# A transformer trunk on one core: first loads joined, the last stage by token, splits by stock in the gated embedding, and a head's output product in the step of its turn

## The chip, the core and the metric

The kernel runs on one core of a Trainium2 chip. The metric is device time in microseconds; the time of a kernel is the median of its runs. Lines such as L226 are lines of the kernel before; the changed kernel has its own numbers, mostly a little higher.

A core has engines that each take their own instructions strictly in order: TensorE (PE: matmuls and transposes), VectorE (DVE), ScalarE (ACT: functions and copies), GpSimd (POOL) and SyncE (SP: here it only issues DMAs). They wait for one another by semaphores.

## The reference, cut to what matters

256 tokens of 1024 channels pass two layers. Each layer has an FFN, a token mixer, a second FFN and a gated embedding; the mixer is latent attention (MLA) in layer 0 and forgetting attention (FoX) in layer 1, with 8 heads each.

```
h = x
for i in range(2):
    h = h + 0.5 * swiglu(rms_norm(h, ffn_norm[i, 0]), ffn_w_in[i, 0], ffn_w_out[i, 0])
    u = rms_norm(h, mix_norm[i])
    h = h + (mla_mixer(u, ...) if i == 0 else fox_mixer(u, ...))
    h = h + 0.5 * swiglu(rms_norm(h, ffn_norm[i, 1]), ffn_w_in[i, 1], ffn_w_out[i, 1])
    gate = sigmoid(rms_norm(h, ple_norm[i]) @ ple_w_gate[i])
    h = h + gate * (p[i] @ ple_w_proj[i])
return rms_norm(h, final_norm)
```

`swiglu` is `(silu(u @ w_in[:, :2816]) * (u @ w_in[:, 2816:])) @ w_out`. All data are float32.

## The kernel before, in words

**State and precision.** The state h lies transposed in `hT`: 8 blocks (d) of 128 channels by 256 tokens. Every large product is made of three matmuls: weights and inputs are each split in a high part and a remainder, and high·high, low·high and high·low are added (`mm3`, `part`, L210–227). With two halves of the input side by side one weight block takes a matmul of 512 columns (`whi`) and one of 256 (`wlo`).

**Weights.** They stream through one plan in the order of use (class `Weights`, L61–136): SP loads a slab of 512 KB into one of 4 raw tiles, ACT makes `whi` (L97), DVE makes `wlo` (L101), and up to 7 such pairs wait for PE. Each call of `W.pump` (L107) splits one more slab at that place of the program; `catch_up` (L121) does so only if fewer than 4 are in stock. So the calls set where the 1 us pieces of ACT and DVE stand among the other work of these engines.

**Norms.** `Norm` (L252–314) never waits before a product: it multiplies the state by the gain and splits it (`high` on ACT, `low` on DVE, both into `u`), while ACT squares each block and POOL adds the squares up. `by_token` (L297) sums them over partitions on PE (`pst`), and takes the root by a power on POOL (`rtok`); `by_column` (L307) spreads it over partitions on PE (`pb`) and ACT copies it (`rb`). The results are scaled by it only after the product.

**First stage.** L834–846 load: the gains, the state in five pieces and the first four slabs, of which the first comes in two halves, on SP's and ACT's queues; 20 matmuls on zeros follow on PE (L848–852), then the loop of L853–862 splits state and slabs, with one square for each of the 8 blocks. `first` multiplies the first four groups block by block as they arrive.

**Attention** (L405–526). Each step h of a loop works on several heads at once, `lag` steps apart (3 in MLA, 2 in FoX): DVE normalizes the shares of head h−2, PE makes the queries of a later head (`project`), multiplies the shares' transposes with the values of head h−lag−1 (`values`: product `po`, L449/450, whose result is split into `os` by ACT and DVE, L206/207), transposes the shares of head h−lag (`turn`: `pt`, which ACT copies to `ptS`, L442–444) and makes the scores of head h−1 (`psc`), whose maximum DVE takes (`nm`) and whose exps ACT makes (`pr`, L427/428). The output projection is filled in between (`fill`): PE adds the products of finished heads to the first 4 output blocks. A table, `MLA_FILLS` or `FOX_FILLS`, says how many such pairs stand at the first and the second place of each step. The order of the loop body:

```
for h in range(H + lag):
    shares(h - 2); project(h, 0)
    fill_some(fills.get((h, 0), 0))
    values(h - lag - 1); turn(h - lag); scores(h - 1)
    project(h, 1); W.catch_up()
    fill_some(fills.get((h, 1), 0))
    ready = h - lag
values(H - 1)
```

**Gated embedding** (`ple`, L754–831). The embedding of the tokens is projected (`pe`, to `es`), then for each block d PE makes the gate (`ps`), DVE scales it (`zg`), ACT takes the sigmoid, DVE splits the block before (`u`) and one slab (`wlo`), and multiplies and adds. In the last layer the same function also squares the new state, transposes it times the final gain back to token order (`po`, 128 by 512), scales it by the root and stores four pieces of 256 KB from SP (L820–831).

Of the kernel before, what the change touches and what calls it, by code (L numbers as in the profile page):

```python
# [19 lines left out]
P = 128  # L20
# [19 lines left out]
G_KV = 74  # L40


MLA_FILLS = {(6, 1): 3, (7, 1): 3, (8, 0): 3, (8, 1): 4, (9, 0): 4, (9, 1): 4, (10, 1): 3}
# [16 lines left out]
class Weights:  # L60
# [60 lines left out]
    def catch_up(self):  # L121

        if self.loaded < self.got + self.PAIRS - 3:
            self.pump()
# [16 lines left out]
def trunk(ctx, tc, xT, pT, pos, gains, freq, bf, ffn_first, ffn_in, ffn_out, w_down, w_uq, w_ukv, mla_o,  # L141
          fox_qk, fox_v, fox_f, fox_o, ple_gate, ple_proj, out):
# [19 lines left out]
    def plan_ple(i):  # L162
        plan.extend(ple_proj[i, c] for c in range(2))
        plan.extend(ple_gate[i, d] for d in range(KD))
# [8 lines left out]
    plan_ple(0)  # L173
# [6 lines left out]
    plan_ple(1)  # L180


    hT = const.tile([P, KD, T], F32, name="hT")
    g_sb = const.tile([P, 75], F32, name="g_sb")
# [67 lines left out]
    class Norm:  # L252


        def __init__(self, gain, blocks, dim, tag="u"):
            self.gain, self.dim, self.acc, self.left = gain, dim, None, blocks
            if gain is not None:
                bufs = 2 if tag == "u" else 1
                self.pair = act.tile([P, blocks, 2, T], F32R, name=tag, bufs=bufs)
# [15 lines left out]
        def square(self, src, cuts=(slice(0, T),)):  # L275
# [3 lines left out]
            self.left -= 1  # L279
            if self.acc is None:  # L280
                self.acc = sq
            elif self.gain is None and self.left == 0:
                self.rest = sq
# [11 lines left out]
        def by_token(self):  # L295
            pst = psm.tile([P, 2], F32, name="pst", tag="small")
            accs = [self.acc] if self.gain is not None else [self.acc, self.rest]  # L297
            for t in range(2):
                for a in accs:
                    nc.tensor.matmul(pst[:, t:t + 1], a[:, t * P:(t + 1) * P], ones[:, :1],  # L300
                                     start=a is accs[0], stop=a is accs[-1])
# [103 lines left out]
    def attention(project, score, v, scale, nxt, lag, fills, early, cumq=None):  # L405
        os = act.tile([P, H, 2, T], F32R, name="os", tag="u")
# [90 lines left out]
        for h in range(H + lag):  # L497
            if 0 <= h - 2 < H:
                shares(h - 2)
            if h < H:  # L500
                project(h, 0)
            elif h == H:
                W.pump()
            fill_some(fills.get((h, 0), 0))
            if 0 <= h - lag - 1:
                values(h - lag - 1)
            if 0 <= h - lag:
                turn(h - lag)
            if 0 <= h - 1 < H:
                scores(h - 1)  # L510
# [27 lines left out]
    def mla(norm, nxt):  # L538
# [48 lines left out]
        queries(0, 1)  # L587
        W.pump()
        nkv.by_token()
# [164 lines left out]
    def ple(pp, norm, nxt):  # L754
        whole = slice(0, T),

        def gated(d, z, e):
            zg, sg, ge = tmp("zg"), tmp("sg"), tmp("ge")

            final = po and d == KD - 1  # L760
            cuts = (slice(0, P), slice(P, T)) if final else whole
            src = hT[:, d, :]
            for c in cuts:
                nc.vector.tensor_mul(zg[:, c], z[:, c], norm.rb[:, c])
            for c in cuts:
                nc.scalar.activation(sg[:, c], zg[:, c], AF.Sigmoid)
            if not po and d:
                nxt.low(d - 1, hT[:, d - 1, :])
            if d < KD - 1:
                W.pump()  # L770
            for c in cuts:
                nc.vector.tensor_mul(ge[:, c], e[:, c], sg[:, c])
                nc.vector.tensor_add(src[:, c], src[:, c], ge[:, c])
            if po:
                nxt.square(src, cuts)
                hg = work.tile([P, T], F32, name="hg", tag="pr", bufs=4)
                for c in cuts:
                    nc.scalar.activation(hg[:, c], src[:, c], AF.Copy, scale=g_sb[:, G_FIN + d:G_FIN + d + 1])
                hgs.append(hg)
            elif d < KD - 1:  # L780
# [6 lines left out]
        def by_token(d):  # L787
            for t in range(2):
                if d % 4 == 0:
                    po[t].append(bank("po", (P, 4 * P)))  # L790
                nc.tensor.transpose(po[t][d // 4][:, d % 4 * P:(d % 4 + 1) * P], hgs[d][:, t * P:(t + 1) * P], ident)


        hgs = []
        po = ([], []) if nxt.gain is None else None

        es = big.tile([P, KD, T], F32, name="es", tag="big")
        for c in range(2):
            w, = W.get()
            for i in range(4):  # L800
                if i % 2 == 0:
                    pe = bank("pe")
                if (c, i) == (1, 2):
# [7 lines left out]
            W.pump()  # L811
        for d in range(KD):
# [3 lines left out]
            if po and d >= 3:  # L816
                by_token(d - 3)
        if po:
            by_token(KD - 3)
            by_token(KD - 2)  # L820
# [262 lines left out]
```

## Time and profile before

| what | us |
|---|---|
| median of 3 runs | 1010.28 (1009.68 to 1011.18) |
| the profiled execution | 1010.07 |
| its span, first to last instruction | 1008.1 |
| PE busy | 992.8 |
| DVE busy | 745.9 |
| ACT busy | 520.7 |
| POOL busy | 435.8 |

2.0 us of the profiled execution lie outside its span. The kernel reads 176.89 MB and writes 1.05 MB, 177 GB/s over the span. Timeline rows give start, duration, engine, line, operation and tiles, and in brackets how long the engine had been idle before and what it waited for. Ends of matmuls are modelled, so the distance from one start to the next tells more than a duration.

### The profile page before, as it was taken

The page shows a single profiled execution, that of the slowest core. Times are in us where ns is not written, and L with a number is a line of the kernel's source. Part 1 is how long each engine was busy: PE and PEld are TensorE (multiplying, and loading weights), DVE is VectorE, ACT ScalarE, POOL GpSimd, SP SyncE. Part 2 cuts the span into 40 slices and gives each one's busy share as a digit, 9 for nine tenths or more (in the row PEclk, how much of TensorE's full clock was granted, in tenths as well). Part 3 has the DMA queues.
Part 4 walks back from the last instruction along what each step waited for, and adds up shares of the span by engine and source line. Part 5 has one row for each costly group of instructions (what it writes and reads, how often), then busy time and mean ns, then how long its engine had stood idle before and what let it go on. Part 6 is the DMA issues. An engine that isn't in the chain of part 4 may idle for free.

```text
span 1008.1 us, 16281 instructions
## 1 busy us (share of the span) xinstructions
PE 992.8 (98%) x6050; PEld 882.0 (87%) x6050; DVE 745.9 (74%) x1057; ACT 520.7 (52%) x836; POOL 435.8 (43%) x360
## 2 busy tenths in 40 slices
PE   8999999999999999999999999999999999999997
PEld 6888888998988888889888888899889888888896
DVE  6777879776768787666877876666877778786665
ACT  6455544466645544445555444446555555454454
POOL 3777731110267765111477673211211577761112
PEclk9999999999999999999999999999999999999998
DMA  7566666542356666665456666556543566666641
GB/s 264 176 209 209 192 179 199 188 162 90 90 184 209 190 189 188 187 198 166 167 174 203 189 184 191 179 193 203 158 147 96 177 211 195 190 183 191 193 165 42
DMA packets 51534, 178.99 MB, mean 178 GB/s; under 512 B 6016, under 2 KB 6400, under 8 KB 51456
## 3 DMA queue, kind: packets, MB, share of 16 engines
q1 hardware_dynamic: 50736, 177.00, 55.8%
q10 hardware_dynamic: 720, 0.96, 0.4%
q8 instruction: 48, 0.79, 0.3%
q14 instruction: 30, 0.25, 0.1%
HBM read 176.89 MB, written 1.05 MB: 177 GB/s over the span
## 4 chain that ended last, share of the span: by engine, by line
PE 90%; DVE 5%; ACT 2%; issue 1%; DMA 1%; POOL 1%; SPq 0%; POOLq 0%; DVEq 0%; ACTq 0%
PE po L226 16%; PE pu L226 16%; PE pg L226 16%; PE po L227 8%; PE pu L227 8%; PE pg L227 8%; PE ps L226 4%; PE ps L227 2%; DVE wlo L101 2%; PE ps L213 1%; PE ps L211 1%; PE ps L212 1%; DVE u L272 1%; PE pv L211 1%; PE pv L213 1%
## 5 line engine op out<-in xcount | busy, mean ns | idle before, releaser
L101 DVE TENSOR_TENSOR wlo<-raw,whi 128x1024 fp32r<-128x1024 f32 (+2 forms) x338 | 418.8, 1248 | 6.7 <-ACT whi L97 6.5
L97 ACT ACTIVATE whi<-raw 128x1024 fp32r<-128x1024 f32 (+2 forms) x338 | 335.4, 1026 | 22.5 <-DMA raw<-in_ffn_in_dram 12.1
L326 POOL TENSOR_TENSOR gu<-two 128x256 f32<-128x256 f32 x176 | 235.9, 1341 | 119.4 <-DVE two L324 110.1
L226 PE MATMUL pg<-u,whi 128*128 128x512 f32 x704 | 251.9, 395 | 3.6 <-DVE u L272 2.3
L226 PE MATMUL pu<-u,whi 128*128 128x512 f32 x704 | 251.2, 395 | 0.0
L226 PE MATMUL po<-hs,whi 128*128 128x512 f32 x704 | 246.3, 394 | 0.0
L227 PE MATMUL pg<-u,wlo 128*128 128x256 f32 x704 | 198.8, 282 | 0.8 <-DVE wlo L101 0.8
L227 PE MATMUL po<-hs,wlo 128*128 128x256 f32 x704 | 198.1, 281 | 0.0
L227 PE MATMUL pu<-u,wlo 128*128 128x256 f32 x704 | 198.0, 281 | 0.0
L226 PEld LDWEIGHTS pg<-u,whi 128*128 128x128 f32 x704 | 132.2, 188 | 35.2 <-DVE u L272 3.3
L226 PEld LDWEIGHTS po<-hs,whi 128*128 128x128 f32 x704 | 132.2, 188 | 30.4
L226 PEld LDWEIGHTS pu<-u,whi 128*128 128x128 f32 x704 | 132.3, 188 | 29.9
L286 POOL TENSOR_TENSOR acc<-acc,sq 128x256 f32<-128x256 f32 x53 | 57.1, 1077 | 188.6 <-ACT sq L278 188.3
L227 PEld LDWEIGHTS pg<-u,wlo 128*128 128x128 f32 x704 | 132.5, 188 | 2.4 <-DVE wlo L101 1.9
L227 PEld LDWEIGHTS pu<-u,wlo 128*128 128x128 f32 x704 | 132.5, 188 | 0.0
L227 PEld LDWEIGHTS po<-hs,wlo 128*128 128x128 f32 x704 | 132.5, 188 | 0.0
L206 ACT ACTIVATE hs<-hid 128x256 fp32r<-128x256 f32 x88 | 36.8, 418 | 142.9 <-POOL hid L344 140.9
L344 POOL TENSOR_TENSOR hid<-sg,gu 128x256 f32<-128x256 f32 x88 | 104.4, 1187 | 6.9
L207 DVE TENSOR_TENSOR hs<-hid,hs 128x256 fp32r<-128x256 f32 x88 | 63.9, 727 | 47.5 <-ACT hs L206 47.5
L324 DVE TENSOR_TENSOR two<-pg,rb 128x512 f32<-128x512 f32 x88 | 60.3, 685 | 49.3 <-PE pg L227 40.5
L267 ACT ACTIVATE u<-hT,g_sb 128x256 fp32r<-128x256 f32 x57 | 29.0, 508 | 130.8 <-DVE hT L387 109.2
L338 ACT ACTIVATE sg<-gu 128x256 f32<-128x256 f32 x88 | 36.8, 418 | 80.1 <-POOL gu L326 80.1
(224 smaller groups left out, 1236.6 us busy)
## 6 DMA issues: line engine op xcount, KB each, us to landing
raw<-in_ffn_in_dram SPq DMA_DIRECT2D x172, 512.0 KB, 3.7
raw<-in_ffn_out_dram SPq DMA_DIRECT2D x64, 512.0 KB, 3.7
raw<-in_ffn_out_dram SPq DMA_DIRECT2D x32, 384.0 KB, 3.7
raw<-in_ple_gate_dram SPq DMA_DIRECT2D x16, 512.0 KB, 4.5
raw<-in_fox_qk_dram SPq DMA_DIRECT2D x16, 512.0 KB, 3.5
raw<-in_mla_o_dram SPq DMA_DIRECT2D x8, 512.0 KB, 3.6
raw<-in_fox_o_dram SPq DMA_DIRECT2D x8, 512.0 KB, 3.6
raw<-in_fox_v_dram SPq DMA_DIRECT2D x6, 512.0 KB, 4.5
```

The costliest lines, as they stand in the source:

```text
L97: self.nc.scalar.activation(self.pairs[i][0][:, c], self.raws[i][:, c], AF.Copy)
L101: self.nc.vector.tensor_sub(lo[:, c], self.raws[i][:, c], hi[:, c].bitcast(F32))
L206: nc.scalar.activation(hi, src, AF.Copy)
L207: nc.vector.tensor_sub(lo, src, hi.bitcast(F32))
L226: nc.tensor.matmul(ps, hi, x[:, k], start=k == 0, stop=False)
L227: nc.tensor.matmul(ps[:, 1, :], lo, x[:, k, 0, :], start=False, stop=k == last)
L267: nc.scalar.activation(self.pair[:, b, 0, c], src[:, c], AF.Copy, scale=g)
L286: nc.gpsimd.tensor_add(new, self.acc, sq)
L324: nc.vector.tensor_mul(two, ps, norm.rb2)
L326: nc.gpsimd.tensor_add(gu[c, i], two[:, 0, :], two[:, 1, :])
L338: nc.scalar.activation(sg, gu.pop((c, 0)), AF.Silu)
L344: nc.gpsimd.tensor_mul(hid[c], gu.pop((c, 0)), gu.pop((c, 1)))
```

## The change

1. *First loads.* Gains and state lie in one array and one tile, `state`, which SP alone loads in three pieces (592, 512 and 1024 columns), alternating with whole slabs. The state in token order (`tokens`, 2 × 512 KB) comes too, behind the next two slabs; two squares with a running sum on ACT over it replace the first norm's 8 squares, 7 POOL additions and its sums on PE. The matmuls on zeros are 22 instead of 20.
2. *MLA prelude.* `nkv.by_token` stands ahead of the pump; `by_column` and the scaling of the keys behind the first value product.
3. *Attention.* `values(h - lag)` stands at the end of the step of its turn, instead of in the next step behind the fills. In MLA the turn stands ahead of the projection. Two fills of MLA move from the second to the first place of their steps.
4. *Gated embedding, layer 0.* Two splits instead of one behind each projection slab; one block later for `by_column`; in the loop `catch_up(3)` instead of `pump`, so that a slab is split only if fewer than three are in stock.
5. *Last stage.* A function of its own, `ple_by_token`: the inputs are stationary and the gate's weights move, 512 columns at a time, so that gate, embedding and state are in token order. The state is transposed ahead of the gate; the root scales inside ACT's sigmoid; the squares are summed by ACT; the final gain is loaded as a row into all partitions. Half of the stores are issued from ACT.

```diff
-MLA_FILLS = {(6, 1): 3, (7, 1): 3, (8, 0): 3, (8, 1): 4, (9, 0): 4, (9, 1): 4, (10, 1): 3}
+MLA_FILLS = {(6, 0): 3, (7, 0): 3, (8, 0): 3, (8, 1): 4, (9, 0): 4, (9, 1): 4, (10, 1): 3}
...
-    def catch_up(self):
+    def catch_up(self, n=PAIRS - 3):
-        if self.loaded < self.got + self.PAIRS - 3:
+        if self.loaded < self.got + n:
             self.pump()
...
         def by_token(self):
-            pst = psm.tile([P, 2], F32, name="pst", tag="small")
...
+            pst = self.sums
+            if pst is None:
+                pst = psm.tile([P, 2], F32, name="pst", tag="small")
...
     def attention(project, score, v, scale, nxt, lag, fills, early, cumq=None):
+        late = lag > 2
...
-            if h < H:
+            if h == H:
+                W.pump()
+            if h < H and not late:
                 project(h, 0)
-            elif h == H:
-                W.pump()
             fill_some(fills.get((h, 0), 0))
-            if 0 <= h - lag - 1:
-                values(h - lag - 1)
             if 0 <= h - lag:
                 turn(h - lag)
+            if h < H and late:
+                project(h, 0)
             if 0 <= h - 1 < H:
                 scores(h - 1)
             if h < H:
                 project(h, 1)
             W.catch_up()
             fill_some(fills.get((h, 1), 0))
+            if 0 <= h - lag:
+                values(h - lag)
             if h >= H:
                 W.catch_up()
-            ready = h - lag
-        values(H - 1)
+            ready = h - lag + 1
...
         queries(0, 1)
+        nkv.by_token()
         W.pump()
-        nkv.by_token()
...
-        nkv.by_column()
-        for i in range(H // 2):
-            nc.vector.tensor_mul(kT[:, 2 * i:2 * i + 2, :], pk[i], nkv.rb2)
...
+                if t == c == 0:
+                    nkv.by_column()
+                    for i in range(H // 2):
+                        nc.vector.tensor_mul(kT[:, 2 * i:2 * i + 2, :], pk[i], nkv.rb2)
...
             if d < KD - 1:
-                W.pump()
+                W.catch_up(3)
...
-                if (c, i) == (1, 2):
+                if (c, i) == (1, 3):
                     norm.by_column()
...
-            W.pump()
+            W.pump(2)
...
+    def ple_by_token(pp, norm):
+        fin = big.tile([P, 5, D], F32, name="fin", tag="big")
+        es, h, gain = fin[:, :2, :], fin[:, 2:4, :], fin[:, 4, :]
+        nc.sync.dma_start(gain, gain_row.to_broadcast([P, D]))
...
+        def gated(t, ps, a, i):
+            sg = work.tile([P, N], F32, name="sgr", tag="pair2", bufs=4)[:, :a.stop - a.start]
+            nc.scalar.activation(sg, ps, AF.Sigmoid, scale=norm.rtok[:, t:t + 1])
+            nc.vector.tensor_mul(sg, es[:, t, a], sg)
+            nc.vector.tensor_add(h[:, t, a], h[:, t, a], sg)
+            nc.scalar.activation(sg, h[:, t, a], AF.Square, accum_out=sums[:, t, i:i + 1])
+            nc.vector.tensor_mul(es[:, t, a], h[:, t, a], gain[:, a])
+        def store(t, n):
...
+            nc.vector.reduce_sum(s, sums[:, t, :n], axis=AX.X)
+            nc.vector.tensor_scalar(v, s, 1.0 / D, EPS, op0=ALU.mult, op1=ALU.add)
+            nc.gpsimd.tensor_tensor(r, v, mhalf[:, :1], op=ALU.pow)
+            nc.scalar.activation(h[:, t, half[0]], es[:, t, half[0]], AF.Copy, scale=r)
+            nc.vector.tensor_scalar(h[:, t, half[1]], es[:, t, half[1]], r, None, op0=ALU.mult)
+            for e, a in zip((nc.scalar, nc.sync), half):
+                e.dma_start(out[t * P:(t + 1) * P, a], h[:, t, a])
...
+        for t in range(2):
+            gated(t, ps[t], half[0], 0)
+        for t in range(2):
+            cuts = [half[1]] if t == 0 else [slice(N, N + N // 2), slice(N + N // 2, D)]
+            for i, a in enumerate(cuts):
...
+                gated(t, last, a, 1 + i)
+            store(t, 1 + len(cuts))
...
+    for i, n in enumerate((2, 2, 4, 0)):
+        if n:
+            b = GAINS + (2, 4, 8)[i] * T
+            nc.sync.dma_start(state[:, a:b], xT[:, a:b])
+            a = b
         nc.sync.dma_start(slabs[:, i, :], ffn_first[i])
+    for t in range(2):
+        nc.sync.dma_start(*W.raw())
+    for t in range(2):
+        nc.sync.dma_start(tokens[:, t, :], xt[t])
     W.fetch()
...
-        n0.square(hT[:, k, :])
...
+            if k == 0:
+                n0.sums = const.tile([P, 2], F32, name="sums")
+                for t in range(2):
+                    nc.scalar.activation(tokens[:, t, :], tokens[:, t, :], AF.Square,
+                                         accum_out=n0.sums[:, t:t + 1])
```

How this moves instructions is seen in three places. The first is PE's order in MLA's loop before the change, from the product of head 2 (step 6) through the turn of head 3, the scores of head 5 (`psc`) to the first of three fills (`ps_2720` is an output block; a pair of rows is one fill):

```order
L449 MATMUL po<-ptS,kqv 128x256
L450 MATMUL po<-ptS,kqv 128x128
L442 MATMUL pt<-ident,pr 128x128 x3
L628 MATMUL psc<-kqv 128x128
L628 MATMUL psc<-kqv 128x256
L530 LDWEIGHTS identb
L530 MATMUL psc<-cmask,identb 128x2x128
L631 MATMUL psc<-kr,kqv 128x128
L631 MATMUL psc<-kr,kqv 128x256
L226 MATMUL ps_2720<-os,whi 128x512
L227 MATMUL ps_2720<-os,wlo 128x256
L226 MATMUL ps_2720<-os,whi 128x512
```

These fills stand behind the scores and read heads 0 and 1 only. After the change PE's order there, from the same product of head 2 (now the end of step 5):

```order
L447 MATMUL po<-ptS,kqv 128x256
L448 MATMUL po<-ptS,kqv 128x128
L228 MATMUL ps_2668<-os,whi 128x512
L229 MATMUL ps_2668<-os,wlo 128x256
L228 MATMUL ps_2668<-os,whi 128x512
L229 MATMUL ps_2668<-os,wlo 128x256
L228 MATMUL ps_2668<-os,whi 128x512
L229 MATMUL ps_2668<-os,wlo 128x256
L440 MATMUL pt<-ident,pr 128x128 x3
L628 MATMUL psc<-kqv 128x128
```

The fills have moved directly behind the product, ahead of the turn and the scores, and the third pair reads head 2, the product of the first two rows. The second place is ACT's order at these steps after the change, from the copy of one head's product (`os<-po`) to that of the second next:

```order
L208 ACTIVATE os<-po 128x256
L442 ACTIVATE ptS<-pt 128x384
L425 ACTIVATE pr,den<-psc,nm,qscale 128x128
L426 ACTIVATE pr,den<-psc,nm,qscale 128x256
L98 ACTIVATE whi<-raw 128x1024
L208 ACTIVATE os<-po 128x256
L442 ACTIVATE ptS<-pt 128x384
L425 ACTIVATE pr,den<-psc,nm,qscale 128x128
L426 ACTIVATE pr,den<-psc,nm,qscale 128x256
L208 ACTIVATE os<-po 128x256
```

The rows have the same order as before the change: the copy still stands behind the exps of a later head, and in every second step behind a `whi`. The third place is DVE's order in the gated embedding's loop of layer 0, blocks 0 to 2, after the change:

```order
L758 TENSOR_TENSOR zg<-ps,rb 128x256
L764 TENSOR_TENSOR ge<-es,sg 128x256
L765 TENSOR_TENSOR state<-state,ge 128x256
L758 TENSOR_TENSOR zg<-ps,rb 128x256
L272 SCALAR_TENSOR_TENSOR u<-state,u 128x256
L764 TENSOR_TENSOR ge<-es,sg 128x256
L765 TENSOR_TENSOR state<-state,ge 128x256
L758 TENSOR_TENSOR zg<-ps,rb 128x256
L272 SCALAR_TENSOR_TENSOR u<-state,u 128x256
L764 TENSOR_TENSOR ge<-es,sg 128x256
```

Before the change each of these blocks also had a `wlo<-raw,whi 128x1024` ahead of `ge`; it stands now only in blocks 3 to 6.

More of the change, by code (lines that the diff above doesn't have):

```diff
@@ L172, in trunk @@
     plan_ffn(1)
-    plan_ple(0)
+    plan_ple()
     plan_ffn(2)
@@ L255, in __init__ @@
         def __init__(self, gain, blocks, dim, tag="u"):
[L256 to L259, printed above, removed]
+            self.gain, self.dim, self.acc, self.sums = gain, dim, None, None
+            self.pair = act.tile([P, blocks, 2, T], F32R, name=tag, bufs=2 if tag == "u" else 1)
         def high(self, b, src, vector=False, cuts=(slice(0, T),)):
@@ L295, in by_token @@
         def by_token(self):
-            pst = psm.tile([P, 2], F32, name="pst", tag="small")
[L297 to L301, printed above, removed]
+            pst = self.sums
+            if pst is None:
+                pst = psm.tile([P, 2], F32, name="pst", tag="small")
+                for t in range(2):
+                    nc.tensor.matmul(pst[:, t:t + 1], self.acc[:, t * P:(t + 1) * P], ones[:, :1], start=True,
+                                     stop=True)
             v = work.tile([P, 2], F32, name="v")
@@ L754, in ple @@
     def ple(pp, norm, nxt):
-        whole = slice(0, T),
         def gated(d, z, e):
             zg, sg, ge = tmp("zg"), tmp("sg"), tmp("ge")
-            final = po and d == KD - 1
-            cuts = (slice(0, P), slice(P, T)) if final else whole
             src = hT[:, d, :]
[L763 to L767, printed above, removed]
+            nc.vector.tensor_mul(zg, z, norm.rb)
+            nc.scalar.activation(sg, zg, AF.Sigmoid)
+            if d:
                 nxt.low(d - 1, hT[:, d - 1, :])
             if d < KD - 1:
-                W.pump()
[L771 to L780, printed above, removed]
+                W.catch_up(3)
+            nc.vector.tensor_mul(ge, e, sg)
+            nc.vector.tensor_add(src, src, ge)
+            if d < KD - 1:
                 nxt.high(d, src)
@@ L846, in trunk @@
+    for t in range(2):
+        nc.sync.dma_start(tokens[:, t, :], xt[t])
     W.fetch()
@@ L850, in trunk @@
     cold = bank("cold", (P, T))
-    for _ in range(20):
+    for _ in range(22):
         nc.tensor.matmul(cold, warm[:, :P], warm, start=True, stop=True)
+    half = [slice(0, 4 * P), slice(4 * P, 8 * P)]
     for k in range(KD):
```

120 lines of the change are left out of this document (70 added, 50 removed).

## The prediction

> **What bounds the kernel now.** I read the page's busy times first, then PE's (TensorE's) waits, then the timeline around each wait and around the places that the change touches. The first fence has the span and the busy time of each engine, and from the view of PE's waits the costliest row of each kind (total, times, longest).
>
> ```profile
> span 1008.1 us, 16281 instructions
> PE 992.8 (98%) x6050; PEld 882.0 (87%) x6050; DVE 745.9 (74%) x1057; ACT 520.7 (52%) x836; POOL 435.8 (43%) x360
> PE pg L226 <- DVE u L272: 2.3, 1, 2.3
> PE pb L310 <- POOL rtok L305: 1.4, 3, 0.6
> PE po L449 <- ACT ptS L444: 0.9, 1, 0.9
> ```
>
> PE is busy for 98% of the span, and every engine takes its instructions in order. So the time is PE's stream of matmuls plus its few waits, and whatever lets PE wait longer is paid in full: no later stage has slack from which to give it back. The next two rows give the rate of that stream: a pair of matmuls with one weight block (512 columns of `whi`, 256 of `wlo`) starts every 950.17 − 949.82 = 0.35 us (0.347 over longer stretches).
>
> ```profile
> 949.82 0.39 PE L226 MATMUL po<-hs,whi 128*128 128x512 f32 x1
> 950.17 0.40 PE L226 MATMUL po<-hs,whi 128*128 128x512 f32 x1
> ```
>
> The profiled execution took 1010.07 us, 0.2 below the median of 1010.28; I work against its own time.
>
> **First loads.** The rows are the stretches (us, busy time of PE, ACT, DVE, POOL and SP, granted clock, DMA share, GB/s) and the timeline of the first block.
>
> ```profile
> 2.00:4.00 2.00, 2.00 (x11) 1.42 (x10) 0.00 (x0) 0.66 (x3) 0.00 (x0) 1.00 0.72 217
> 4.00:6.00 2.00, 1.43 (x8) 0.76 (x5) 0.48 (x1) 0.69 (x3) 0.00 (x0) 1.00 0.78 227
> 8.00:10.00 2.00, 1.17 (x5) 0.60 (x4) 1.18 (x2) 1.84 (x4) 0.84 (x1) 1.00 1.04 415
> 5.37 0.63 ACT L97 ACTIVATE whi<-slabs 128x512 fp32r<-128x512 f32 x1 [1.31 <-DMA slabs<-in_ffn_first_dram]
> 6.05 0.50 PE L226 MATMUL pg<-u,whi 128*128 128x512 f32 x1 [0.62 <-ACT whi L97]
> 8.82 0.50 PE L226 MATMUL pg<-u,whi 128*128 128x512 f32 x1 [0.60 <-ACT whi L97]
> 14.53 0.39 PE L227 MATMUL pg<-u,wlo 128*128 128x256 f32 x1 [0.37 <-DVE wlo L101]
> 20.28 0.39 PE L226 MATMUL pg<-u,whi 128*128 128x512 f32 x1
> ```
>
> From 6.05 to 20.28 PE runs 32 pairs, which need 32 × 0.347 = 11.1 us; it takes 14.23, the waits of 0.60 and 0.37 shown among it. So at most 3.1 us can be saved behind the first matmul. The change sends the state and whole slabs in rows of 2 to 4 KB on one queue, in the order of use, and takes eight squares and seven POOL additions out of this stretch. The first matmul now needs 303 + 512 KB, about 815 KB; by 5.37 the old kernel had moved 2 × 0.217 + 1.37 × 0.227 = 0.75 MB since 2.00. With some quickening from the longer rows I leave the first matmul at 6.0. The second slab and its state (774 KB more) then come at near 0.4 MB/us, so by about 8 us, when PE still has work until 9; the third and fourth follow ahead of need. That leaves the stretch at 6.0 + 11.1 + 0.5 = 17.6: **−2.6**. If the old rate of 0.22 lasts to 8 us, the first matmul comes at 6.4 and the second slab holds PE for another 0.8: −1.4. If all goes well: −3.2. The token rows (1 MB, 2.5 us at 0.4 MB/us) come ahead of the third raw tile; their sums are needed only when the first block's results are scaled, behind 17.6, so I cost them at nothing; without that cover they would add up to 0.6.
> The Trainium skill's "DMA: Bandwidth & Descriptors", in "Issuing engines are not separate DMA queues", says that transfers started by several engines share the same 16 DMA engines, and that a second issuer saves only the sequencer's issue time. By it, giving up the ACT queue neither frees nor costs bandwidth, and the early rate would stay at the 217 to 227 GB/s of the rows: this term would then be about −1.7. No run here separates the two yet.
>
> **MLA prelude.** `by_token` goes ahead of the pump and `by_column` behind the first `psv` product, which covers this wait (0.17 for the loads, 0.3 by the spacing): **−0.3** (−0.2 to −0.4).
>
> ```profile
> 213.88 0.71 PE L310 MATMUL pb<-ident,rtok 128*128 128x128 f32 x4 [0.17 <-POOL rtok L305]
> ```
>
> **The attention loop of MLA.** This is the largest term. The rows show head 2's product, the next turn, and what ScalarE (ACT) and VectorE (DVE) do until that product's split is ready; then the first turn of the loop.
>
> ```profile
> 236.27 0.70 PE L449 MATMUL po<-ptS,kqv 128*128 128x256 f32 x2
> 237.03 0.49 PE L442 MATMUL pt<-ident,pr 128*128 128x128 f32 x3
> 238.12 0.46 ACT L427 ACTIVATE pr<-psc,nm,qscale 128x128 f32<-128x128 f32 x1 [1.90 <-DVE nm L418]
> 239.11 1.05 ACT L97 ACTIVATE whi<-raw 128x1024 fp32r<-128x1024 f32 x1
> 240.05 0.37 ACT L206 ACTIVATE os<-po 128x256 fp32r<-128x256 f32 x1
> 240.46 0.42 DVE L207 TENSOR_TENSOR os<-po,os 128x256 fp32r<-128x256 f32 x1 [0.47 <-ACT os L206]
> 240.86 0.70 PE L449 MATMUL po<-ptS,kqv 128*128 128x256 f32 x2 [0.88 <-ACT ptS L444]
> 224.65 0.47 PE L211 MATMUL ps<-q,whi 128*128 128x256 f32 x1
> 225.91 0.35 DVE L436 TENSOR_SCALAR pr<-pr,inv 128x256 f32<-128x256 f32 x1
> 226.29 0.49 PE L442 MATMUL pt<-ident,pr 128*128 128x128 f32 x3
> ```
>
> The product holds PE until 237.03, 0.7 us; its split is complete at 240.46 + 0.42 = 240.88, 4.6 us after the product began, since on ACT the `os` copy queues behind two exps and, in every second step, a `whi` of 1.05. In the old kernel the output product's partial sums (the fills) that read this head come a step later, so PE never sees those 4.6 us. In the new order they stand directly behind the product: three fills in step 6, of which the third reads head 2. Ahead of it lie the product's 0.7 and two fills of 0.35, 1.4 in all: PE waits 4.6 − 1.4 = 3.2 us. In step 7 the first fill reads head 3, produced just before; without the `whi` its split takes 4.6 − 1.05 = 3.6, less the product's 0.7: 2.9. In step 8 the third fill reads head 4, with `whi`: 3.2 again. Behind each waiting fill PE's queue holds the next turn and scores, so the whole chain of heads slips with it. Walking the loop's instructions through the four queues with the durations of the rows, the scores come a little earlier relative to the product, and I get 3.0 + 2.4 + 2.65, and 0.4 for head 5: 8.4.
> Turn 0 now stands ahead of the second-next projection, which began at 224.65 and filled the time until the shares were ready at 225.91 + 0.35 = 226.26: that is 226.29 − 224.65 = 1.6 more on PE (1.5 in the walk, which has a short wait there already). What goes: the waits for `ptS`, of which the trace shows 0.88 and the walk 2.2 in the old order and 0.3 in the new. Sum: 8.4 + 1.5 − 1.9 = **+8.0**. The lower end, 6.5, takes 0.5 less for each of the three large waits, if ACT comes to the copy earlier; the upper end, the simple sums of 3.2 + 2.9 + 3.2 + 1.6, less only the 0.88 shown and with 0.4 for head 5, is 9.4.
>
> **FoX's loop.** Here the turn's order stays, and only one fill, the second of step 9, meets a head whose product has just begun. The rows give that head's time from product to split: 764.58 + 0.42 − 763.31 = 1.7. The product and the fill ahead cover 0.65 + 0.35, so **+0.7** (0.3 to 1.2).
>
> ```profile
> 763.31 0.59 PE L449 MATMUL po<-ptS,kqv 128*128 128x256 f32 x2
> 764.16 0.39 ACT L206 ACTIVATE os<-po 128x256 fp32r<-128x256 f32 x1 [2.20 <-PE po L450]
> 764.58 0.42 DVE L207 TENSOR_TENSOR os<-po,os 128x256 fp32r<-128x256 f32 x1 [2.79 <-ACT os L206]
> ```
>
> **Gated embedding of layer 0.** `by_column` comes one block later, which covers the wait of the first row: **−0.7** (−0.5 to −0.8; 0.61 shown, 0.77 by the spacing). The rest is DVE's: the gate's first operation `zg` at the loop's second and last block, the split `wlo` between them, and PE's wait at the end of the loop.
>
> ```profile
> 461.17 0.71 PE L310 MATMUL pb<-ident,rtok 128*128 128x128 f32 x4 [0.61 <-POOL rtok L305]
> 469.06 0.42 DVE L764 TENSOR_TENSOR zg<-ps,rb 128x256 f32<-128x256 f32 x1 [0.42 <-PE ps L213]
> 485.88 0.42 DVE L764 TENSOR_TENSOR zg<-ps,rb 128x256 f32<-128x256 f32 x1
> 486.94 1.22 DVE L101 TENSOR_TENSOR wlo<-raw,whi 128x1024 fp32r<-128x1024 f32 x1
> 489.40 0.42 DVE L764 TENSOR_TENSOR zg<-ps,rb 128x256 f32<-128x256 f32 x1
> 490.60 0.50 PE L226 MATMUL pg<-u,whi 128*128 128x512 f32 x1 [2.35 <-DVE u L272]
> ```
>
> A block takes PE 24 matmuls, 2.87 us, but DVE 489.40 − 485.88 = 3.52, `wlo` included; from the second block on (on time at 469.06) it falls behind to 489.40 − (469.06 + 6 × 2.87) = 3.1 us at the last. The new loop has `wlo` in four blocks instead of seven, and DVE is on time when they begin: 4 × 0.65 = 2.6, less some 0.3 of slack, 2.3. The wait of 2.35 shrinks by the difference: **−0.8** (−0.5 to −1.5). What it moves, two splits ahead of the loop, falls into DVE's idle time there, so I cost them at nothing; they cost 1.2 each if `zg` waits for them.
>
> **Last stage.** The rows are the last matmul of the gate, the root, the scaling and the stores.
>
> ```profile
> 998.36 0.28 PE L213 MATMUL ps<-u,whi 128*128 128x256 f32 x1
> 1001.55 0.70 POOL L305 TENSOR_TENSOR rtok<-v,mhalf 128x2 f32<-128x2 f32 x1 [2.77 <-DVE v L303]
> 1002.28 1.26 ACT L828 ACTIVATE o<-po,rtok 128x512 f32<-128x512 f32 x2 [0.86 <-POOL rtok L305]
> 1003.00 1.82 SPq L831 DMA_DIRECT2D out_dram<-o  x4
> ```
>
> Gate and embedding have the same columns to multiply, now with 512 moving instead of 256 (two thirds of a pair, 0.231 each). The four matmuls of `pb` (0.7 us, as at 461.17) go and 16 transposes stay; no term is worth more than that 0.7. Behind the last gate matmul (end 998.64) the old kernel takes 1008.07 − 998.64 = 9.4 us. The new tail has no sum over partitions on PE, and half of the stores leave earlier; but sigmoid, square and scaling of the second half of the tokens stand in one ACT queue with the first half's. I take 9.0 for it, with 8.2 and 10.0 as ends. Together **−1.1** (−2.0 to +0.3).
>
> **Sum.** −2.6 − 0.3 + 8.0 + 0.7 − 0.7 − 0.8 − 1.1 = +3.2, so 1010.07 + 3.2 = 1013.3 us.
>
> **The rivals.** *The splits come in time* (the other side, faster). If ACT takes the `os` copy ahead of the exps and the `whi`, as its 0.37 us would allow, the split is ready 0.7 + 0.37 + 0.42 = 1.5 us after the product began, and the three waits fall to 0.1, 0.8 and 0.1. The loop is then 1.0 + 1.5 − 1.9 = +0.6 and the kernel, with the other terms' −4.8, at about 1006. It decides the sign once the three waits together stay under 3 us, so that the loop costs less than 2.8: the copy would have to start some 1.7 us earlier than it does. For it: ACT is busy only 52%. Against: the rows above show the copy 3.8 us behind the product, behind work that the new order leaves ahead of it. Chance 0.17.
> *Gains and losses cancel.* With the loop at its lower end, 6.5, and the start at −3.2, the tail at −2.0 and the gated loop at −1.5, the sum is 6.5 + 0.3 − 3.2 − 0.3 − 0.7 − 1.5 − 2.0 = −0.9; milder mixes give 0 to +2: about 1010.5, within the bound. That the first loads don't come sooner at all, since the same bytes and 1 MB more go through the same engines, would not lead here: it would put 2.6 back on the forecast, near 1016. Chance 0.23.
> *The clock falls.* If waits of 2.4 to 3 us let PE's granted clock drop, the matmuls behind them run slower. The stretch behind the old wait of 2.35 us shows full clock (PE's busy time, clock, DMA share, GB/s):
>
> ```profile
> 496.70:500.00 3.30, 3.30 (x22) 1.00 0.91 346
> ```
>
> A drop to half for 4 us behind two of the waits would add about 4: 1017. Chance 0.04. The Trainium skill's "TensorE: Matmul & The Clock Gate", in "Part 1: The HAM clock gate", puts the idle time that halves the clock at about 3.4 us; by that the three waits would stay just below it.
>
> **How the numbers follow.** The forecast, 1013.3, has the remaining 0.56. About 0.2% (2.0 us, 1008.3 to 1012.3) is what a measurement of this kernel can tell from no change. The forecast's own spread, from the ends of its terms, is 1011 to 1016; below 1012.3 it gives 0.05 to "same". So faster 0.17, same 0.27, slower 0.56. The range takes in most of the cancelling case and leaves out the clock and the first rival: 1008.5 to 1016.3.
>
> **What would show it.** In the new profile PE should wait three times for DVE's `os` at the fills of MLA, 2.4 to 3 us each, with a `whi` or exps on ACT between product and copy; turn 0 should wait about 1.6 for the shares; the first block's 32 pairs should end near 17.6; the wait behind the gated loop should be near 1.5. The prediction is wrong if the fills wait less than 1 us each, if the first block ends at 20 as before, or if the tail behind the last gate matmul exceeds 10 us.

## The result and the profile after

The changed kernel takes 1017.21 us (median of 5 runs, 1015.34 to 1019.81) against 1011.18 before (5 runs, 1009.68 to 1011.85): a ratio of 1.0064, interval 1.0045 to 1.0083, slower by 6.0 us. (The median of 1010.28 given ahead of the prediction is that of the first three of the five runs before.) The direction was forecast, the size was not: 1013.3 was forecast, with 1016.3 as the upper end. The profiled execution took 1017.48 us, with a span of 1015.4.

PE's waits after the change, in the same view as before (what waited for what, total us, times, longest):

```profile
PE ps L228 <- DVE os L209: 8.3, 5, 2.8
PE pg L228 <- DVE u L272: 1.5, 1, 1.5
PE pt L440 <- DVE pr L433: 1.1, 1, 1.1
PE pg L228 <- ACT whi L98: 0.8, 1, 0.8
```

The first row is new: the fills of the attention loops wait for the split `os` of a head just produced. `pb`'s three waits are gone, and the wait behind the gated embedding has shrunk. The next rows show the first of the new waits, with what ACT and DVE do meanwhile (timeline of the changed kernel):

```profile
234.46 0.59 PE L447 MATMUL po<-ptS,kqv 128*128 128x256 f32 x2
235.46 0.39 PE L228 MATMUL ps<-os,whi 128*128 128x512 f32 x1
235.98 0.46 ACT L425 ACTIVATE pr<-psc,nm,qscale 128x128 f32<-128x128 f32 x1 [2.17 <-DVE nm L416]
236.97 1.05 ACT L98 ACTIVATE whi<-raw 128x1024 fp32r<-128x1024 f32 x1
237.91 0.38 ACT L208 ACTIVATE os<-po 128x256 fp32r<-128x256 f32 x1
238.32 0.43 DVE L209 TENSOR_TENSOR os<-po,os 128x256 fp32r<-128x256 f32 x1 [1.33 <-ACT os L208]
238.80 0.51 PE L228 MATMUL ps<-os,whi 128*128 128x512 f32 x1 [2.83 <-DVE os L209]
```

From the product at 234.46 to the end of the split at 238.75 it is 4.3 us; PE does two fills and then stands still. By the distance of starts this wait costs 2.99 us (the brackets count idle time only, 2.83). The other new waits in the loops, and the smaller one behind the gated embedding:

```profile
223.37 0.61 PE L440 MATMUL pt<-ident,pr 128*128 128x128 f32 x3 [1.13 <-DVE pr L433]
245.70 0.50 PE L228 MATMUL ps<-os,whi 128*128 128x512 f32 x1 [2.21 <-DVE os L209]
254.17 0.50 PE L228 MATMUL ps<-os,whi 128*128 128x512 f32 x1 [2.45 <-DVE os L209]
259.53 0.50 PE L228 MATMUL ps<-os,whi 128*128 128x512 f32 x1 [0.23 <-DVE os L209]
771.28 0.50 PE L228 MATMUL ps<-os,whi 128*128 128x512 f32 x1 [0.58 <-DVE os L209]
498.19 0.50 PE L228 MATMUL pg<-u,whi 128*128 128x512 f32 x1 [1.54 <-DVE u L272]
```

By the distance of starts they are 1.40, 2.37, 2.61, 0.39, 0.74 and 1.70 us. What the sum of these does not hold is seen in the stretches of the loop (us, PE's busy time, granted clock, DMA share, GB/s). The granted clock is the share of PE's full clock that the profile records; the stretches are cut where that record changes, every 3.41 us, and are called windows from here on:

```profile
235.86:239.27 3.41, 0.58 (x4) 1.00 0.33 72
239.27:242.68 3.41, 3.41 (x15) 0.50 0.20 82
242.68:246.09 3.41, 1.21 (x7) 1.00 0.00 0
246.09:249.51 3.42, 3.42 (x14) 0.50 0.00 0
249.51:252.92 3.41, 2.22 (x14) 1.00 0.00 0
```

Behind the first two long waits PE ran at half of its clock, each time for 3.41 us, in which it did the work of 1.7: another 3.4 us. The whole of MLA's loop is measured from the start of the second product `psv` (the values, ahead of the loop) to the first matmul of the FFN behind it. The first two rows are of the kernel before, the others of the changed kernel:

```profile
215.14 0.39 PE L211 MATMUL psv<-whi,kv 128*128 128x512 f32 x1
269.87 0.39 PE L226 MATMUL pg<-u,whi 128*128 128x512 f32 x1
212.27 0.48 PE L213 MATMUL psv<-whi,kv 128*128 128x512 f32 x1
279.03 0.39 PE L228 MATMUL pg<-u,whi 128*128 128x512 f32 x1
```

That is 54.7 us before and 66.8 after: +12.0 where +8.0 was forecast, and 8.6 without the 3.4 of the clock.

The start and the last stage went the other way. The start, as windows with the same columns as before:

```profile
2.00:4.00 2.00, 2.00 (x12) 1.46 (x11) 0.00 (x0) 0.51 (x3) 0.00 (x0) 1.00 0.91 320
4.00:6.00 2.00, 1.18 (x10) 0.77 (x8) 0.75 (x2) 1.14 (x3) 0.00 (x0) 1.00 1.02 340
```

The first matmul behind the 32 pairs of the first loads, called the start of the third block below, for which the kernel before has 20.28:

```profile
18.30 0.39 PE L228 MATMUL pg<-u,whi 128*128 128x512 f32 x1
```

The last stage runs from its first matmul to the end of the span:

```profile
976.50 0.39 PE L213 MATMUL pe<-whi,q 128*128 128x512 f32 x1
1006.44 0.28 PE L215 MATMUL ps<-wlo,u 128*128 128x256 f32 x1
```

That is 1015.36 − 976.50 = 38.9 us, against 1008.07 − 967.29 = 40.8 before. PE's part went from 31.4 to 30.2, the tail behind the last matmul of the gate from 9.4 to 8.6.

### The profile page after: what moved, and what is told of

Its sections match the earlier page's. It is cut to its first block, busy times and chain, and to the rows that moved or that the text cites. A ratio compares the mean times of both kernels' runs of the same rounds, so it can differ in the third digit from the quotient of the medians.

```text
span 1015.4 us, 16002 instructions
## 1 busy us (share of the span) xinstructions
PE 993.2 (98%) x5940; PEld 877.1 (86%) x5940; DVE 741.9 (73%) x1050; ACT 517.2 (51%) x821; POOL 424.7 (42%) x348
## 4 chain that ended last, share of the span: by engine, by line
PE 92%; DVE 4%; ACT 2%; issue 1%; DMA 1%; SPq 0%; POOLq 0%; POOL 0%; ACTq 0%
PE po L228 16%; PE pu L228 16%; PE pg L228 16%; PE po L229 8%; PE pu L229 8%; PE pg L229 8%; PE ps L228 5%; PE ps L229 2%; PE ps L215 1%; PE ps L214 1%; PE ps L213 1%; DVE wlo L102 1%; PE pv L213 1%; PE pv L215 1%; PE pv L214 1%
## 5 line engine op out<-in xcount | busy, mean ns | idle before, releaser
L228 PEld LDWEIGHTS pu<-u,whi 128*128 128x128 f32 x704 | 132.3, 188 | 30.2
L283 POOL TENSOR_TENSOR acc<-acc,sq 128x256 f32<-128x256 f32 x42 | 47.1, 1121 | 174.9 <-ACT sq L278 174.7
L209 DVE TENSOR_TENSOR hs<-hid,hs 128x256 fp32r<-128x256 f32 x88 | 63.5, 722 | 48.6 <-ACT hs L208 48.6
L267 ACT ACTIVATE u<-state 128x256 fp32r<-128x256 f32 x57 | 29.0, 508 | 130.8 <-DVE state L384 109.1
```

Source lines behind the costliest of these rows:

```text
L209: nc.vector.tensor_sub(lo, src, hi.bitcast(F32))
L228: nc.tensor.matmul(ps, hi, x[:, k], start=k == 0, stop=False)
L267: nc.scalar.activation(self.pair[:, b, 0, c], src[:, c], AF.Copy, scale=g)
```

## The experiments

The theory after this reading: the fills that read a head just produced make PE wait as worked out, and the idle PE loses its clock on top of that. Rivals: the matmuls behind the waits are slow for another reason; the turn ahead of the projection is what costs; another part of the change loses time too.

**Zeros in the waits.** Matmuls on zeros, which add nothing to the sums, stand ahead of the three waiting fills:

```diff
+PAD = {(0, 2): 24, (0, 3): 19, (1, 4): 21}
...
-                part(pss[d], ws[d], os, range(upto[d], n), H - 1)
+                for k in range(upto[d], n):
+                    for _ in range(PAD.get((d, k), 0) if late else 0):
+                        nc.tensor.matmul(pss[d][:, 0, :], warm[:, :P], warm, start=False, stop=False)
+                    part(pss[d], ws[d], os, range(k, k + 1), H - 1)
```

> The changed kernel with 24, 19 and 21 matmuls on zeros (0.11 us each) put on TensorE ahead of the three fills of MLA that wait for a split; they add zero to the sums and fit into the waits of 2.99, 2.37 and 2.61 us. Theory of the clock (idle TensorE loses its clock: half of full speed for 3.4 us twice behind these waits, 1.7 us each): no stretch of the loop is below full clock, the end of the loop comes 3.4 us earlier, about 1013.8 us. Rival (the matmuls behind the waits are slow for another reason, such as copies from the same banks or transfers): the slow stretches stay and the time stays at 1017. Rival of mere delay: if the zeros do not fit, slower than 1017.

Measured: 1014.28 us (1013.81 to 1015.52), ratio to before 1.0032 (1.0020 to 1.0045); 2.9 less than the changed kernel. The loop in this run (us, busy, clock, DMA share, GB/s):

```profile
234.00:250.00 16.00, 15.69 (x115) 1.00 0.12 36
```

The same waits, filled with work that nobody needs, cost no clock: the slow matmuls came from the idle time, and the clock's share of the loss is about 3 us. The fills still come as late as before: MLA's loop takes 63.5 us from `psv` to the FFN, 3.3 less than in the changed kernel and 8.8 more than before the change.

**Fills a head later.** One line, so that no fill reads a head produced in the step before it:

```diff
-            ready = h - lag + 1
+            ready = h - lag
```

> The changed kernel, but the fills of a step may read only the heads that were finished a step earlier, as before the change. Theory of the waits (the three fills directly behind a product cost 8.4 us, and the clock lost behind two of them 3.5): the walk of the loop gives 1.0 us more than before instead of 8.0, no idle time above 1.5 us and no drop of the clock: 1017.2 - 7.0 - 3.5 = about 1006.7 us. Rival (the turn ahead of the projection or the product in the step of its turn is what costs): no more than half of it is won, 1012 or more.

Measured: 1007.20 us (1006.53 to 1008.50), ratio 0.9961 (0.9947 to 0.9974): 10.0 us less than the changed kernel, with 10.5 expected. The waits for `os` are gone, though the turn still stands ahead of the projection and the products still stand in the steps of their turns:

```profile
PE pt L440 <- DVE pr L433: 1.6, 2, 1.1
PE pg L228 <- DVE u L272: 1.5, 1, 1.5
PE pb L307 <- POOL rtok L302: 1.5, 1, 1.5
PE po L447 <- ACT ptS L442: 1.2, 2, 0.6
```

So the readiness of the fills, that `+ 1`, carries most of the loss: 10.0 of the 12.2 us that the next run finds for the whole new loop. The third row is a wait at the first `pb`, which the changed kernel's first trace does not have; more on it below.

**The old loop in the changed kernel.** The loop body and `MLA_FILLS` of before, all else changed.

> The changed kernel with the loop body of attention and the table of fills from before; everything else changed. Theory of the waits and the clock: the loops are as before, and the other four parts give -2.4 (first loads), -0.4 (prelude), -0.7 - 0.8 (gated embedding), -1.1 (last stage): 1017.2 - 11.7 - 0.7 = about 1005, or 5 to 6 below before. Rival (another part of the change loses time too, which the comparison of the traces hides): above 1008.

Measured: 1004.96 us (1003.95 to 1005.76), ratio 0.9936 (0.9924 to 0.9948). The other four parts together gain 6.5 us, and the new loop loses 1017.2 − 1005.0 = 12.2. Whether one of the four loses a little by itself is not seen here; the first loads and the last stage were also run alone (below), the prelude and the gated embedding were not.

**The new loop alone.** The kernel before with the new loop body and table.

> The kernel before with the new loop body and the new table of fills only. Theory of the waits and the clock: +8.0 in MLA, +0.7 in FoX, and one to three drops of the clock of 1.7 us, which depend on where the waits fall in windows of 3.4 us: 1020 to 1024 us. Rival (the loop loses 8 us only together with the other parts): below 1017.

Measured: 1022.00 us (1021.08 to 1022.99), ratio 1.0106 (1.0092 to 1.0120): +10.7 us by the ratio. The loop loses nearly the same without the other parts. In its trace the same three waits brought only one stretch of half clock, behind the second:

```profile
239.78:243.19 3.41, 1.64 (x11) 1.00 0.56 154
243.19:246.60 3.41, 1.38 (x9) 1.00 0.00 0
246.60:250.01 3.41, 3.24 (x12) 0.50 0.00 0
```

**The changed kernel twice more,** unaltered, to see where the clock falls.

> The changed kernel again, unaltered. Theory of windows (the clock is judged in windows of 3.41 us that run on their own, and is halved for one window behind one in which TensorE was idle for most of it): the same three waits of 3.0, 2.4 and 2.6 us in the loop, but the halved windows fall behind others of them than the second and third row of this profile showed, each 3.41 us long and at a distance of whole windows from each other. Rival (the length of the wait decides): half clock behind the waits of 2.99 and 2.37 and never behind that of 2.61, as in the first trace.

> The changed kernel a third time, unaltered, for the same question: where the stretches of half clock fall when the same waits stand at another place of the windows. Theory of windows: a pattern different from at least one of the other two traces. Rival (the length of the wait decides): the same pattern as in the first trace.

Measured: 1014.97 and 1018.57 us, one execution each. The waits are the same (2.99, 2.37 and 2.61 by the distance of starts). The first of the two has one stretch of half clock, the second has two:

```profile
236.56:239.97 3.41, 1.69 (x12) 1.00 0.46 154
239.97:243.38 3.41, 1.33 (x9) 1.00 0.00 0
243.38:246.80 3.42, 3.29 (x12) 0.50 0.00 0
```

```profile
236.96:240.37 3.41, 0.60 (x3) 1.00 0.23 64
240.37:243.78 3.41, 3.41 (x14) 0.50 0.22 90
243.78:247.19 3.41, 1.21 (x7) 1.00 0.00 0
247.19:250.61 3.42, 3.42 (x13) 0.50 0.00 0
```

In the first the wait of 2.99 us fell across the end of a window, each part of it left the window over 1.6 us of work, and the clock stayed. So the length of a wait does not decide alone: its place in windows that run on their own does. The second run's pattern is that of the first trace, as far as windows go. Behind the wait of 2.61 us the clock stayed full in all four traces that have it (the changed kernel's three and the new loop alone); there the windows that it fell in held 1.71 us of work or more.

**First loads alone.** The kernel before with the tile `state`, the new order of loads, the token rows with their two squares, and 22 matmuls on zeros.

> The kernel before with the new first loads, the 22 matmuls on zeros and the squares over the token rows only. Theory of the start (slabs and state come in the order of use and the first block's pairs run almost without waits): -2.0 to -2.6, about 1008.8 us by a before of 1011.2; if the third raw tile comes late behind the token rows in many runs, as one trace showed with a wait of 1.6 us at the first normalization by column, only -1. Rival (the bandwidth is the same, so that the new order wins nothing beyond this profile's luck): no change, 1011.2.

Measured: 1009.46 us (12 runs, 1006.87 to 1010.42), ratio 0.9984 (0.9974 to 0.9993), a gain of 1.6 by the ratio. The single times spread over 3.5 us. Its trace starts the third block at 17.93, near the 17.6 that was forecast, but then waits for the root:

```profile
25.06 0.71 PE L313 MATMUL pb<-ident,rtok 128*128 128x128 f32 x4 [1.37 <-POOL rtok L308]
```

Later it loses its clock behind the wait at the end of the gated embedding, 2.5 us as in the kernel before (stretches, columns as above):

```profile
486.87:490.28 3.41, 1.04 (x7) 1.00 0.44 154
490.28:493.69 3.41, 3.41 (x13) 0.50 0.00 0
```

**State from ACT's queue.** The run with the old loop, with the second and third piece of the state issued by ScalarE:

```diff
-            nc.sync.dma_start(state[:, a:b], xT[:, a:b])
+            (nc.sync if i == 0 else nc.scalar).dma_start(state[:, a:b], xT[:, a:b])
```

> The run with the old loop, but the second and third piece of the state are issued from ScalarE's queue, as the small pieces were before the change; sizes and rows stay. If the rate of the first microseconds (320 GB/s in 2 to 4 us instead of 217) comes from the longer rows, it stays and the time stays near 1005. If it comes from the single queue in the order of use, the rate falls to near 220 and the second and third slab come 1 us late: 1006 to 1007.

Measured: 1004.27 us (1002.80 to 1004.49), ratio 0.9928 (0.9915 to 0.9941), not distinguishable from the run with the old loop. The early rate stays above the old 217 and 227 GB/s:

```profile
2.00:4.00 2.00, 2.00 (x11) 1.00 0.88 294
4.00:6.00 2.00, 1.08 (x10) 1.00 1.03 416
```

The second queue is not what matters; the larger pieces with longer rows go with the higher rate. Which of size and row length it is was not tried, and the gap is smaller than one trace makes it look: between 2 and 4 us the old loads moved 217 GB/s in the kernel before, but 243 and 281 in two other traces (last stage alone, new loop alone).

**Token rows later,** behind four raw tiles instead of two, with the squares one step of `first` later (`if k == 2`), in the run with the old loop.

> The run with the old loop, but the token rows are loaded behind the first four raw tiles instead of between the second and third, and their two squares stand one step of the first block later on ScalarE. Theory of the token rows (1 MB ahead of the third raw tile delays the splits on ScalarE and VectorE, and with them the first root, by 1.5 us in about half of the executions): the wait at the first normalization by column is gone from all of them, and the median falls by 0.5 to 1 below that run's 1005.0, about 1004.3, with a smaller spread. Rival (the rows come too late at their new place): a wait there of 1 us or more in every execution, 1006.

Measured: 1006.88 us (1005.02 to 1007.89), ratio 0.9951 (0.9937 to 0.9964): the rival's 1006, no gain. The rows come too late: `pb` waits longer:

```profile
25.75 0.71 PE L307 MATMUL pb<-ident,rtok 128*128 128x128 f32 x4 [2.37 <-POOL rtok L302]
```

And that idle time costs the clock as well:

```profile
23.84:27.25 3.41, 1.50 (x10) 1.00 0.63 195
27.25:30.66 3.41, 3.41 (x13) 0.50 0.30 113
```

**No token rows,** with the squares and sums of before, in the run with the old loop.

> The run with the old loop and the new order of the first loads, but without the token rows: the first norm's squares on ScalarE and sums on GpSimd are as before the change. If the order and the sizes of the loads carry the gain at the start, it stays as it is or grows a little, since 1 MB less is loaded: 1004 to 1005. If the squares and additions taken out of the first block carry it, VectorE's and ScalarE's splits come late again and the block ends near 20: 1006 to 1007.

Measured: 1005.66 us (1004.84 to 1007.23), ratio 0.9945 (0.9933 to 0.9958), within 0.7 us of the run with the old loop. The third block starts at 19.17, over a microsecond later than with the token rows, and `pb` doesn't wait. So the squares taken out of the first block are worth about that microsecond, and the late third raw tile gives it back in part of the executions. What is left goes with the order and size of the loads and is not large: 19.17 here, against 19.47 to 20.32 in the three traces with the old loads.

**Last stage alone** in the kernel before.

> The kernel before with the new last stage only. By the sum of the prediction: -1.1 us, of which 0.8 is the wait for the root ahead of the gate (not needed any more) and 0.3 the tail: 1010.0 by a before of 1011.1. Rival (the tail in token order, with sigmoid, square and scaling in one queue, is longer than 10 us): no gain, or slower.

Measured: 1008.37 us (6 runs, 1007.26 to 1008.83), ratio 0.9970 (0.9959 to 0.9982), a gain of 3.0 (1.8 to 4.1); the trace has 1006.33 − 967.73 = 38.6 us for the stage, 2.2 less than before. The gain is larger than forecast.

## Why the prediction was wrong

The direction and the waits were forecast rightly. The step that failed is the one by which the clock was left out of the sum: the prediction held that waits of 2.4 to 3 us leave PE's clock full, put the loss at nothing, and gave the rival "the clock falls" a chance of 0.04 at about 4 us, "1017". That rival is what happened: the measured time is 1017.2, two windows of half clock cost 3.4 us in the profiled execution, and filling the waits gave 2.9 back. Of the three signs by which the prediction would have known itself wrong none appeared.

The old wait of 2.35 us, from which the prediction judged the clock, lies in these windows of the kernel before (columns as above):

```profile
486.50:489.91 3.41, 1.75 (x10) 1.00 0.45 153
489.91:493.33 3.42, 2.73 (x15) 1.00 0.31 123
```

The terms of the sum, one by one:

- *The waits of MLA's loop.* Forecast 3.0, 2.4, 2.65 and 0.4 for the fills and 1.5 for turn 0; measured 2.99, 2.37, 2.61, 0.39 and 1.40, and +8.6 for the loop without the clock, where +8.0 was forecast. The walk through the four queues held, since each engine's order was known and the durations were rows. The fills were the cause, as the run with the fills a head later showed. The upper end of this term is added up wrongly: 3.2 + 2.9 + 3.2 + 1.6 − 0.88 + 0.4 is 10.4, not 9.4. The range was thus, if anything, too narrow on the side where the result fell; the clock was missing from it all the same. Two smaller slips change nothing: 20.28 − 17.6 is 2.7, and moving 0.05 to "same" leaves 0.28 and 0.55.
- *The clock.* The prediction took one wait of 2.35 us behind which the clock was full as evidence that waits up to 3 us are free of it. The row that it shows, 496.70 to 500.00, begins 6.1 us behind the end of that wait, later than a halved window of 3.41 us would have ended. The clock was full directly behind it too, but because the wait lay, in that one execution, across the two windows above, with 1.75 and 2.73 us of work. The same wait in two of the experiments' traces with the old gated embedding (first loads alone, last stage alone) fell into one window and cost the clock. The sentence on the Trainium skill's "TensorE: Matmul & The Clock Gate" ("by that the three waits would stay just below it") misled in the same way: the page's section "Part 1: The HAM clock gate" has a free-running window of 3.413 us, and the runs agree with that length to the row; but it speaks of a whole idle window, and here a window with up to 1.55 us of work was enough. The runs decide.
- *First loads.* Forecast −2.6. The third block came 2.0 earlier in the changed kernel's trace, 2.2 to 2.5 in six of the other seven with these loads, and 0.2 in the one that lost its clock there; alone the part gained 1.6. The old start was measured in one execution only: in the run with the last stage alone, which has the old loads, the third block starts at 19.47 instead of 20.28. What failed besides is the sentence that cost the token rows at nothing: in three of eight traces with these loads the first root came 1.5 to 1.6 us late, behind the splits of the third and fourth raw tile, where 0.6 was the worst that the prediction named. The Trainium skill's "DMA: Bandwidth & Descriptors", section "Issuing engines are not separate DMA queues", by which a second issuer saves only issue time, agrees with the run with the state from ACT's queue (1004.27 us against 1004.96); but its use in the prediction, as a reason that the rate would stay, failed: with pieces of another size on one queue the rate was 320 GB/s instead of 217.
- *Prelude and gated embedding.* Forecast −0.3, and −0.7 − 0.8. The `pb` waits are gone and the wait behind the gated embedding fell from 2.51 to 1.70, as forecast; by the stretches the two parts gave −0.5 and −1.3.
- *FoX.* Forecast +0.7, with 1.2 as the upper end. The fill waits 0.74, as forecast, but from the first scores to the FFN behind it FoX takes 790.67 − 714.77 = 75.9 us against 781.47 − 706.98 = 74.5 before, +1.4. The cause of the other 0.7 stays open. In the run with the fills a head later the fill's wait is gone, a turn waits about 0.5 in its place, and FoX takes 75.7.
- *Last stage.* Forecast −1.1, measured −1.9 in the trace, −3.0 (1.8 to 4.1) alone. PE's part gave 1.1 instead of 0.7, and the tail is 8.6 us where 9.0 was taken, within the ends.

Taken together, from one profiled execution to the other: first loads and the first norm −2.4, prelude −0.5, MLA +12.0, gated embedding −1.3, FoX +1.4, last stage −1.9, which make the +7.3 between the two spans. Without the 3.4 of the clock that is +3.9, where +3.2 was forecast. The medians differ by 6.0 only, and the mean granted clock listed with every execution suggests why: one halved window takes 0.0017 off that mean (half of 3.41 us in 1008), and nearly all executions of the kernel before over 1010.5 us have 0.993 to 0.996, those under it 0.996 to 0.998. So the kernel before seems to lose its clock in part of its executions too; the profiled one, from which the prediction worked, did not. No trace of this kernel shows such a window, so this is inferred. Whether the clock answers to the busy time of PE or to something like the rows that it multiplies stays open: the zeros of the first experiment counted as work.

The version without the new loop, at 1005, beats both kernels: the change was worth making except for the new loop.

## What to carry to other kernels

Where one engine sets the time, order each consumer so that its input was finished a step earlier; moving a producer earlier gains nothing if its reader moves with it, and a wait in an in-order queue also holds all that stands behind it. Count what a wait does to the clock as well: a wait of over half a window may cost its own length and 1.7 us more, by chance from run to run, and a spread that grows after a change is a hint of that (2.2 us before, 4.5 after, 1.7 with the zeros in the waits). A price taken from one trace's single lucky wait is no bound.

## What the runs showed of the hardware

The granted clock is set in windows of 3.41 us that run on their own. From the first block to PE's last matmul, the traces have ten windows with 0.58 to 1.55 us of PE's busy time, and in all ten cases the next window had half the clock; behind the windows with 1.64, 1.69, 1.75 and more it did not. Behind each of these halved windows, which held 3.05 to 3.42 us of busy time, the clock was full again. One costs 1.7 us, and its place differs between executions of one kernel: 1014.97, 1017.48 and 1018.57 us were profiled with one, two and two such windows. The bound showed even at the start, where in the run with the state from ACT's queue the first block lost its clock:

```profile
4.02:7.43 3.41, 1.55 (x11) 1.00 1.03 417
7.43:10.84 3.41, 3.33 (x10) 0.50 1.03 418
```
